# Three pieces of the key compression's weights split into places of their own

## Chip, core and metric

One core of a Trainium2 chip runs the whole kernel. The metric is device time in microseconds from launch to end, as a median of runs. Beside it there is one profiled execution, from which all rows below come.

## The reference

One decoder layer over 512 tokens of width 1024, in float32. A normalised input is projected once; the columns of that projection feed an HGRN2 group of heads (a gated linear recurrence) and a sparse-attention group with three branches: compressed, selected and window keys. Both results go through one output projection, then a gated convolutional FFN of width 2816 and a last norm. The part that matters here is the compression of keys and values and what runs next to it:

```python
def compress_blocks(kv, pe, w1, w2):
    ...
    blk = kv[:, tok] + pe[:, None, :].astype(kv.dtype)
    blk = blk.transpose(0, 3, 1, 2, 4).reshape(B, G, n_cmp, CMP_BLOCK * D)
    return jax.nn.silu(blk @ w1) @ w2
...
    kc = compress_blocks(kc_raw, pe_k, ck_w1, ck_w2)
    vc = compress_blocks(kv_heads(v_cmp), pe_v, cv_w1, cv_w2)
```

`w1` is 2048 x 256, so each of the two compressions multiplies a 2 MB weight.

## The kernel before

**Products in two halves.** Every float32 weight is split into a high part in the fp32r type and a low part, the remainder. ScalarE makes the high part (line 129), VectorE the low part (line 130), and TensorE then runs three products (high-high, high-low, low-high) that it adds up in PSUM. In the compression the two parts of the activations lie side by side in one operand, so there are two products for each step (lines 445 and 446).

**Places.** A piece of a weight is 128 x 1024 floats (512 KB). `stage` loads it into one of four places `ws` through SP's DMA queue. `hilo` takes one of four places `wh` and one of four places `wl`. A place `ws` comes free when VectorE's `wl` is done; places `wh` and `wl` come free when TensorE's last product with them is done. So no load starts until an earlier piece is split, and no piece is split until an earlier one is multiplied.

**Names of the pieces**, in the order of the program: KC and VC (keys and values to be compressed, line 400), q0a and q0b (`proj_q(0)`, line 373), K0 (`proj_k(0)`, line 386), then ck0 to ck3 (`compress(0)`, line 441), hi0 and hi1 (`hgrn_nat`, line 621), cv0 to cv3 (`compress(1)`), and then the pieces of the work that fills gaps in the attention. KC to K0 take 24 products of 512 columns each; ck and cv take 8 products of 256 columns for a piece; hi0 and hi1 together 96 products of 256 columns.

**Other tiles.** `xx` is a shifted copy of the roped keys or the values, made by eight DMAs on SP's queue (lines 409 and 410); `xa` and `xs` (lines 418 and 421) are made from it by VectorE and ScalarE and are the left operand of the compression. `khl` (line 384) holds the keys of one group of heads and is filled by four DMAs on SP's queue (line 394). Tag `k` has two places of 128 x 2048 floats: they hold in turn `wvh` (twice, the weights of the values), the `khl` of group 0 and of group 1, and later `kg` of the recurrence. `sg0` and `sg1` are the gates of the HGRN2 group, `mixn0` to `mixn3` the results of the attention.

**Order.** The program's text gives each instruction a priority, and a scheduler that runs while the kernel is built lays down one fixed order for each engine and queue: the first in the text among those that it finds ready. The places of a tag are handed out while it does so. The order around the change is written by hand:

```python
ck, cv, hi = compress(0), compress(1), hgrn_nat(OFF_HI, 0)
for st in (ck, ck, hi, ck, hi, cv, ck, cv, hi, cv, hi, cv):
    next(st, None)
```

Of the kernel before, what the change touches and what calls it, by code (L numbers as in the profile page):

```python
# [8 lines left out]
F32 = mybir.dt.float32  # L9
F32R = mybir.dt.float32r  # L10
# [7 lines left out]
P = 128  # L18
# [3 lines left out]
NT = SEQ // P  # L22
# [7 lines left out]
WSLOT = 1024  # L30
# [25 lines left out]
def kernel(ctx: ExitStack, tc: tile.TileContext, ins, consts: bass.AP, out: bass.AP):  # L56
# [66 lines left out]
    def hilo(n):  # L123
        hi = wp.tile([P, WSLOT], F32R, name="wh", tag="wh")[:, :n]
        lo = wp.tile([P, WSLOT], F32R, name="wl", tag="wl")[:, :n]
        return hi, lo
# [2 lines left out]
        nc.scalar.activation(dst_hi, src, AF.Copy)  # L129
        nc.vector.tensor_tensor(dst_lo, src, dst_hi.bitcast(F32), ALU.subtract)  # L130

    def chunk(src, shape):
        n = shape[0] * shape[1]
        st = stage(src, shape)
        hi, lo = hilo(n)
        split(hi, lo, st)
        v = lambda a: a.rearrange("p (a b) -> p a b", a=shape[0])
        return v(hi), v(lo)
# [69 lines left out]
    with ExitStack() as fc:  # L208
        fp = fc.enter_context(tc.tile_pool(name="fp", bufs=1))
# [159 lines left out]
        def proj_q(g):  # L369
            qt2 = [qp.tile([P, 2, SEQ], F32R, name=f"qs{g}{b}", tag="q") for b in range(2)]  # L370
            qs[g] = [qt2[b // 2][:, b % 2, :] for b in range(NB)]
            for pair in range(2):
                wh, wl = chunk(w_in[:, :, OFF_NQ + 256 * g + P * pair:OFF_NQ + 256 * g + P * (pair + 1)], (KT, P))
                y = rope(proj_T(wh, wl))
                qq = fp.tile([P, 2, SEQ], F32R, name="qq", tag="junk", bufs=3)
                nc.scalar.activation(qq[:, 0, :], y, AF.Copy, scale=0.125)
                nc.vector.scalar_tensor_tensor(qq[:, 1, :], y, 0.125, qq[:, 0, :].bitcast(F32), ALU.mult, ALU.subtract)
                for e in range(2):
                    for r in range(2):
                        nc.sync.dma_start(qt2[pair][r * HD:(r + 1) * HD, e, :].bitcast(F32), qq[e * HD:(e + 1) * HD, r, :].bitcast(F32))  # L380
                yield

        def proj_k(g):
            khl = fp.tile([P, 2, 2, SEQ], F32R, name=f"khl{g}", tag="k", bufs=2)
            kh[g], kl[g] = khl[:, 0], khl[:, 1]
            st = stage([w_in[:, :, off + g * HD:off + (g + 1) * HD] for off in (OFF_KS, OFF_KW)], (KT, P))
            hi, lo = hilo(DM)
            split(hi, lo, st)
            y = rope(proj_T(*(a.rearrange("p (a b) -> p a b", a=KT) for a in (hi, lo))))
            th = fp.tile([P, 2, SEQ], F32R, name="th", tag="junk", bufs=3)  # L390
            split(th[:, 0, :], th[:, 1, :], y)
            for br in range(2):
                for r in (0, HD):
                    nc.sync.dma_start(khl[r:r + HD, :, br, :].bitcast(F32), th[br * HD:(br + 1) * HD].bitcast(F32))
            yield
# [3 lines left out]
        for which, off in enumerate((OFF_KC, OFF_VC)):  # L399
            wh, wl = chunk(w_in[:, :, off:off + P], (KT, P))  # L400
# [29 lines left out]
        own = sm.tile([P, NB], F32, name="own", bufs=1)  # L430
        nc.vector.tensor_reduce(own, ident.rearrange("p (b n) -> p b n", b=NB)[:, :, 0:NCMP], AX.X, ALU.add)

        def compress(which):
            w1n, w2n = (("cmp_k_w1", "cmp_k_w2"), ("cmp_v_w1", "cmp_v_w2"))[which]
            w2 = fp.tile([P, 2, 2, HD], F32, name="w2", tag="w2", bufs=2)
            for r in range(2):
                nc.sync.dma_start(w2[:, :, r, :], ins[w2n][0].rearrange("(k p) d -> p k d", p=P))
            w1 = ins[w1n][0].rearrange("(j p) h -> p j h", p=P)
            hid = bank("pt")[:, :256]
            for c in range(4):  # L440
                wh, wl = chunk(w1[:, 4 * c:4 * c + 4, :], (4, 256))
                for j in range(4):
                    jj = 4 * c + j
                    lhs = kvx[which][jj // 8][:, jj % 8, :]
                    mm(hid, lhs, wh[:, j, :], jj == 0, False)
                    mm(hid, lhs, wl[:, j, :], False, jj == 15)
                if c == 1:
                    yield
            hs = fp.tile([P, 256], F32, name="hs", tag="asq")[:2 * NC2, :]
            nc.scalar.activation(hs, hid[:2 * NC2, :], AF.Copy)  # L450
            yield
            hp = bank("pt")[:, :2 * NC2]
            for m in range(2):
                mm(hp[:, m * NC2:(m + 1) * NC2], hs[:, m * P:(m + 1) * P], cst[:2 * NC2, C_CMB:C_CMB + NC2], True, True)
            th = sm.tile([P, 2 * NC2], F32, name="cth", tag="cth", bufs=2)
            nc.scalar.activation(th, hp, AF.Tanh, scale=0.5)
            nc.vector.scalar_tensor_tensor(th, th, 1.0, hp, ALU.add, ALU.mult)
            if which:
                thr = hw("thr").rearrange("p (a b n) -> p a b n", a=4, b=NB)
                nc.gpsimd.memset(thr, 0.0)  # L460
                nc.scalar.activation(thr[:, :, :, 0:NCMP], th.rearrange("p (a n) -> p a n", a=4).unsqueeze(2).broadcast_to([P, 4, NB, NCMP]), AF.Copy)
            yield
            act = [th[:, m * NC2:(m + 1) * NC2] for m in range(2)]
            if which == 0:
                o = bank("pt")[:, :2 * NCMP]
                for m in range(2):
                    mm(o, w2[:, m].rearrange("p a d -> p (a d)"), act[m], m == 0, m == 1)
                o3 = o.rearrange("p (g n) -> p g n", g=2)
                nc.scalar.activation(kc[:, :, 0, 0:NCMP], o3, AF.Copy, scale=0.5)
                nc.vector.scalar_tensor_tensor(kc[:, :, 1, 0:NCMP], o3, 0.5, kc[:, :, 0, 0:NCMP].bitcast(F32), ALU.mult, ALU.subtract)  # L470
            else:
                for g in range(2):
                    o = bank("pt")[:, :HD]
                    for m in range(2):
                        mm(o, thr[:, 2 * m + g].rearrange("p b n -> p (b n)"), w2[:, m, 0, :], m == 0, m == 1)
                    vf = fp.tile([P, NB, HD], F32, name="vf", tag="asq")
                    nc.vector.scalar_tensor_tensor(vf, o.unsqueeze(1).broadcast_to([P, NB, HD]), 0.5, own.unsqueeze(2).broadcast_to([P, NB, HD]), ALU.mult, ALU.mult)
                    split(vc[:, g, :, 1, :], vc[:, g, :, 0, :], vf)


        mixn = [fp.tile([P, 512], F32, name=f"mixn{t}") for t in range(NT)]


        scaled = {}
# [131 lines left out]
        vh, sg = {}, {}  # L616
# [3 lines left out]
        def hgrn_nat(off, c0):  # L620
            ws = [chunk(w_in[:, 4 * a:4 * a + 4, off + c0:off + c0 + 256], (4, 256)) for a in range(2)]
            pair = c0 // 256
            if off == OFF_HI:
                vh[pair] = fp.tile([P, NT, 256], F32, name=f"vh{pair}", tag="junk", bufs=3)
            else:
                sg[pair] = fp.tile([P, NT, 256], F32, name=f"sg{pair}")
            for t in range(NT):
                o = bank("mm")[:, :256]
                tk = slice(t * P, (t + 1) * P)
                for k in range(KT):  # L630
                    wh, wl = ws[k // 4]
                    mm3(o, hh[:, k, tk], hl[:, k, tk], wh[:, k % 4, :], wl[:, k % 4, :], k == 0, k == KT - 1)
                if off == OFF_HI:
                    nc.scalar.activation(vh[pair][:, t, :], o, AF.Copy)
                else:
                    th = unit("gth")[:, :256]
                    nc.scalar.activation(th, o, AF.Tanh, scale=0.5)
                    nc.vector.scalar_tensor_tensor(sg[pair][:, t, :], th, 1.0, o, ALU.add, ALU.mult)
                yield
# [117 lines left out]
        def attention(g):  # L757
            units = [(g, i, r) for i in TILES[g] for r in ((3, 0) if i < 2 else (1, 2, 0))]
            for u, n in zip(units, FILL[g]):
                pr = softmax_parts(*u)  # L760
                if todo:
                    weighted(*todo.pop())
                todo.append((*u, pr))
                every(itertools.islice(filler, n))
            weighted(*todo.pop())
# [8 lines left out]
# [3 lines that stand above are left out]
        for st in (ck, cv, hi):  # L777
            every(st)
        filler = itertools.chain(proj_q(1), proj_k(1), hgrn_nat(OFF_HG, 0), hgrn_nat(OFF_HG, 256), hgrn_fq(0), hgrn_nat(OFF_HI, 256), hgrn_fq(1))
        attention(0)  # L780
        attention(1)
        every(filler)
# [331 lines left out]
```

## Time and profile before

| | |
|---|---|
| median of 3 runs | 692.2 us (690.06 to 693.33) |
| profiled execution, its own time | 691.09 us |
| its span, first to last instruction | 689.3 us |
| TensorE busy | 672.1 us, 98% of the span |
| mean granted TensorE clock | 0.994 |

The profiled execution lies 1.1 us under the median, within the spread of the runs. 1.8 us of its time lie outside the span. Matmuls are pipelined, so a matmul's duration overlaps the next one's; what a product costs in a dense stream is the distance from one start to the next.

### The profile page before, as it was taken

How to read it: one execution, taken by the hardware profiler on the slowest of the kernel's cores; microseconds unless marked ns; L12 is line 12 of the kernel's file. 1: busy time of each engine (PE TensorE's matmuls, PEld its weight loads, DVE VectorE, ACT ScalarE, POOL GpSimd, SP SyncE). 2: the span in 40 equal slices, each digit the busy share in tenths (PEclk: the TensorE clock that was granted, in tenths of full speed). 3: DMA queues.
4: the chain of work that ended last, by engine and by line, in shares of the span. 5: the costliest groups of instructions: out<-in, count | busy, mean ns of one | idle time of the engine just before them, and what ended most of it. 6: DMA issues, size and time to landing. Idle time of an engine off the chain costs nothing.

```text
span 689.3 us, 11311 instructions
## 1 busy us (share of the span) xinstructions
PE 672.1 (98%) x4357; PEld 589.8 (86%) x4357; DVE 530.1 (77%) x930; ACT 392.4 (57%) x730; POOL 31.1 (5%) x82
## 2 busy tenths in 40 slices
PE   7999999999999999999999999999999999999995
PEld 4988878888888887887999898989989898989884
DVE  6878489887787678856886879788786878778665
ACT  6834587688878556335275464545445453645425
POOL 2000000000020121000000000000000000000001
PEclk9999999999999999999999999999999999999998
DMA  7947942320324312222231334334342333324303
GB/s 245 248 134 194 260 127 63 92 56 8 91 63 129 116 62 62 61 63 61 62 93 47 97 103 121 104 89 117 92 123 83 101 94 100 120 87 123 122 3 122
DMA packets 91142, 71.26 MB, mean 103 GB/s; under 512 B 8007, under 2 KB 78415, under 8 KB 91088
## 3 DMA queue, kind: packets, MB, share of 16 engines
q1 hardware_dynamic: 90800, 70.01, 35.3%
q8 instruction: 34, 0.56, 0.3%
q10 hardware_dynamic: 288, 0.52, 0.2%
q14 instruction: 20, 0.16, 0.1%
HBM read 63.18 MB, written 2.10 MB: 95 GB/s over the span
## 4 chain that ended last, share of the span: by engine, by line
PE 73%; DVE 12%; DMA 4%; ACT 4%; issue 3%; POOL 1%; SPq 1%; POOLq 0%; DVEq 0%; ACTq 0%
PE bmm L81 31%; PE bs L81 15%; PE bpt L81 15%; PE bo L81 8%; DVE wl L130 3%; PE bpt L565 2%; DMA ws<-in_ffn_w_up_dram 2%; POOL rs L110 1%; ACT wh L129 1%; DMA ws<-in_cmp_v_w_dram 1%; DVE x L993 1%; ACT y L1060 1%; DMA qs<-qq 1%; DMA xx<-y 1%; PE bpt L185 1%
## 5 line engine op out<-in xcount | busy, mean ns | idle before, releaser
L130 DVE TENSOR_TENSOR wl<-ws,wh 128x1024 fp32r<-128x1024 f32 x108 | 118.7, 1107 | 42.2 <-ACT wh L129 41.3
L129 ACT ACTIVATE wh<-ws 128x1024 fp32r<-128x1024 f32 x108 | 103.9, 964 | 60.1 <-PE bmm L81 21.4
L81 PE MATMUL bmm<-hTh,wh 128*128 128x256 f32 (+1 forms) x416 | 134.7, 324 | 0.0
L81 PE MATMUL bmm<-hTh,wl 128*128 128x256 f32 (+1 forms) x416 | 134.7, 324 | 0.0
L81 PE MATMUL bmm<-hTl,wh 128*128 128x256 f32 (+1 forms) x416 | 133.8, 322 | 0.6 <-DVE hTl L130 0.6
L81 PE MATMUL bs<-tt,wh 128*128 128x256 f32 x456 | 84.6, 284 | 0.2 <-ACT bs L961 0.2
L81 PEld LDWEIGHTS bmm<-hTl,wh 128*128 128x128 f32 x416 | 78.4, 189 | 6.6 <-DVE hTl L130 0.8
L81 PEld LDWEIGHTS bmm<-hTh,wl 128*128 128x128 f32 x416 | 78.4, 188 | 6.1 <-DVE wl L130 0.4
L81 PEld LDWEIGHTS bmm<-hTh,wh 128*128 128x128 f32 x416 | 78.4, 188 | 5.8
L129 ACT ACTIVATE wh<-s 128x1024 fp32r<-128x1024 f32 x38 | 40.4, 1064 | 58.8 <-PE bpt L81 24.8
L81 PEld LDWEIGHTS bs<-tt,wh 128*128 128x128 f32 x456 | 70.4, 188 | 2.3 <-ACT bs L961 0.4
L81 PE MATMUL bpt<-wh,ah 128*128 128x512 f32 (+1 forms) x179 | 70.4, 393 | 0.5 <-DVE x L993 0.5
L81 PE MATMUL bpt<-wl,ah 128*128 128x512 f32 (+1 forms) x179 | 70.0, 391 | 0.0
L81 PE MATMUL bpt<-wh,al 128*128 128x512 f32 (+1 forms) x179 | 70.0, 391 | 0.0
L81 PE MATMUL bs<-tt,wl 128*128 128x256 f32 x228 | 63.8, 280 | 0.0
L81 PE MATMUL bmm<-wh,hTh 128*128 128x256 f32 (+1 forms) x192 | 63.1, 330 | 0.2 <-DVE y L361 0.2
L81 PE MATMUL bmm<-wl,hTh 128*128 128x256 f32 (+1 forms) x192 | 62.7, 327 | 0.0
L81 PE MATMUL bmm<-wh,hTl 128*128 128x256 f32 (+1 forms) x192 | 61.9, 323 | 0.0
L130 DVE TENSOR_TENSOR wl<-s,wh 128x1024 fp32r<-128x1024 f32 x38 | 46.5, 1224 | 18.2 <-ACT wh L129 17.9
L110 POOL TENSOR_TENSOR rs<-ms,mhalf 128x4 f32<-128x4 f32 (+1 forms) x23 | 19.0, 828 | 587.9 <-DVE ms L108 587.9
L81 PEld LDWEIGHTS bs<-tt,wl 128*128 128x128 f32 x228 | 43.0, 189 | 0.0
L81 PEld LDWEIGHTS bpt<-wh,ah 128*128 128x128 f32 x179 | 33.6, 188 | 8.3 <-DVE x L993 1.3
(262 smaller groups left out, 1373.7 us busy)
## 6 DMA issues: line engine op xcount, KB each, us to landing
ws<-in_w_in_dram SPq DMA_DIRECT2D x22, 512.0 KB, 4.2
ws<-in_ffn_w_gate_dram SPq DMA_DIRECT2D x22, 512.0 KB, 4.0
ws<-in_ffn_w_up_dram SPq DMA_DIRECT2D x22, 512.0 KB, 4.3
ws<-in_ffn_w_down_dram SPq DMA_DIRECT2D x20, 512.0 KB, 3.7
ws<-in_w_o_dram SPq DMA_DIRECT2D x8, 512.0 KB, 3.4
ws<-in_cmp_k_w_dram SPq DMA_DIRECT2D x4, 512.0 KB, 4.6
qs<-qq SPq DMA_DIRECT2D x16, 128.0 KB, 3.4
ws<-in_cmp_v_w_dram SPq DMA_DIRECT2D x4, 512.0 KB, 6.1
```

What stands on the lines that cost most here:

```text
L81: return nc.tensor.matmul(o, lhsT, rhs, start=start, stop=stop, skip_group_check=True)
L110: nc.gpsimd.tensor_tensor(rs[:, :width], ms[:, :width], mhalf[:, :width], ALU.pow)
L129: nc.scalar.activation(dst_hi, src, AF.Copy)
L130: nc.vector.tensor_tensor(dst_lo, src, dst_hi.bitcast(F32), ALU.subtract)
L185: nc.tensor.transpose(pt[:, j * P:(j + 1) * P], self.y[:, c:c + P], ident)
L565: t = nc.tensor.transpose(pt[:, b * P:(b + 1) * P], srcs[b], ident)
L993: nc.vector.tensor_tensor(x_sb[t][:, hs], o, x_sb[t][:, hs], ALU.add)
L1060: nc.scalar.activation(y[:, HV[h]], y[:, HV[h]], AF.Copy, scale=rs)
```

## The change

The high and low parts of ck0, ck1 and ck2 no longer take places `wh` and `wl`. ck0 takes one place of a tag `sg` and one of a tag `mixn`; so does ck1; ck2 takes the two halves of a place of tag `k`. ck3 and all pieces of the value compression stay as they were. `sg0` and `sg1` get a common tag with two places, and the four `mixn` tiles become two tiles of double width in two places, made just before the attention. The bytes set aside are the same as before.

```diff
-    def chunk(src, shape):
+    def chunk(src, shape, room=None):
         n = shape[0] * shape[1]
         st = stage(src, shape)
-        hi, lo = hilo(n)
+        hi, lo = room or hilo(n)
         split(hi, lo, st)
...
+        def room(which, c):
+
+            if which or c == 3:
+                return None
+            if c == 2:
+                both = fp.tile([P, 2, WSLOT], F32R, name="wk", tag="k", bufs=2)
+                return both[:, 0], both[:, 1]
+            return [fp.tile([P, WSLOT], F32R, name="wk", tag=t, bufs=2) for t in ("sg", "mixn")]
+
         def compress(which):
...
-                wh, wl = chunk(w1[:, 4 * c:4 * c + 4, :], (4, 256))
+                wh, wl = chunk(w1[:, 4 * c:4 * c + 4, :], (4, 256), room(which, c))
...
-        mixn = [fp.tile([P, 512], F32, name=f"mixn{t}") for t in range(NT)]
+        mixn = []
...
-                sg[pair] = fp.tile([P, NT, 256], F32, name=f"sg{pair}")
+                sg[pair] = fp.tile([P, NT, 256], F32, name=f"sg{pair}", tag="sg", bufs=2)
...
+        for _ in range(2):
+            m2 = fp.tile([P, 2, 512], F32, name="mixn", tag="mixn", bufs=2)
+            mixn += [m2[:, 0], m2[:, 1]]
         attention(0)
```

## Rows read from the trace of the kernel before

**Rows 1.** Busy time by stretch of the compression and its neighbours: stretch in us from the span's start, its length, then busy us and instructions of each engine, granted clock, DMA share, GB/s.

```profile
30.00:45.00 15.00, 15.00 (x66) 12.09 (x65) 9.04 (x22) 4.81 (x8) 0.00 (x0) 1.00 0.71 195
45.00:60.00 15.00, 14.76 (x82) 12.51 (x80) 14.97 (x26) 8.28 (x12) 0.53 (x1) 1.00 0.49 137
60.00:65.00 5.00, 4.11 (x24) 3.81 (x24) 3.49 (x5) 1.82 (x3) 0.00 (x0) 0.78 0.85 241
65.00:70.00 5.00, 5.00 (x40) 5.00 (x39) 3.16 (x4) 1.95 (x5) 0.00 (x0) 0.88 0.69 154
```

**Rows 2.** TensorE's matmuls in order of time: start, us, line, output and inputs, moving operand, count; in brackets the idle time before and what ended it. `bpt<-wh,xs` is a product of a compression, `bmm<-wh,hTh` one of hi0 or hi1. From 55.42 to 59.05 there are 32 starts, from 62.74 to 66.28 there are 18.

```profile
55.42 0.28 PE L81 MATMUL bpt<-wh,xs 128*128 128x256 f32 x1
...
59.05 0.28 PE L81 MATMUL bpt<-wl,xs 128*128 128x256 f32 x1
59.16 0.40 PE L81 MATMUL bmm<-wh,hTh 128*128 128x256 f32 x2
59.80 0.66 PE L81 MATMUL bpt<-cst,hs 124*128 124x62 f32 x4 [0.24 <-ACT hs L450]
60.68 0.38 PE L81 MATMUL bmm<-wh,hTh 128*128 128x256 f32 x1 [0.22 <-DVE y L361]
61.73 0.35 PE L81 MATMUL bpt<-wh,xs 128*128 128x256 f32 x1 [0.67 <-issue]
61.92 0.28 PE L81 MATMUL bmm<-wl,hTh 128*128 128x256 f32 x1
...
62.74 0.36 PE L81 MATMUL bmm<-wh,hTl 128*128 128x256 f32 x1
...
66.28 0.28 PE L81 MATMUL bmm<-wl,hTh 128*128 128x256 f32 x1
...
76.93 0.28 PE L81 MATMUL bmm<-wl,hTh 128*128 128x256 f32 x1
77.69 0.39 PE L81 MATMUL bpt<-wh,xs 128*128 128x256 f32 x1 [0.48 <-ACT wh L129]
```

**Rows 3.** VectorE in order of time, same columns: the six low parts `wl` are those of ck0, ck1, ck2, ck3, hi0 and hi1, in this order; between them stand the last step of a rope (line 363; the one at 36.47 is that of KC) and the last splits of `xs`.

```profile
36.47 0.70 DVE L363 TENSOR_TENSOR y<-y,sh 128x512 f32<-128x512 f32 x1
39.68 1.23 DVE L130 TENSOR_TENSOR wl<-ws,wh 128x1024 fp32r<-128x1024 f32 x1 [2.52 <-ACT wh L129]
...
49.16 1.25 DVE L130 TENSOR_TENSOR xs<-xa,xs 128x496 fp32r<-128x496 f32 x2
...
50.93 1.22 DVE L130 TENSOR_TENSOR wl<-ws,wh 128x1024 fp32r<-128x1024 f32 x1
52.07 0.69 DVE L363 TENSOR_TENSOR y<-y,sh 128x512 f32<-128x512 f32 x1
52.67 1.22 DVE L130 TENSOR_TENSOR wl<-ws,wh 128x1024 fp32r<-128x1024 f32 x1
...
56.97 1.22 DVE L130 TENSOR_TENSOR wl<-ws,wh 128x1024 fp32r<-128x1024 f32 x1
...
60.54 1.21 DVE L130 TENSOR_TENSOR wl<-ws,wh 128x1024 fp32r<-128x1024 f32 x1
...
62.27 1.22 DVE L130 TENSOR_TENSOR wl<-ws,wh 128x1024 fp32r<-128x1024 f32 x1
```

**Rows 4.** ScalarE in order of time, same columns: high parts (line 129, `wh`): at 38.59 that of ck0, at 55.44 those of ck3 and hi0, at 64.40 that of cv1, at 69.79 that of cv2; and two that stand behind one (line 406 takes the values out of PSUM, `th` are the keys of group 0).

```profile
38.59 1.06 ACT L129 ACTIVATE wh<-ws 128x1024 fp32r<-128x1024 f32 x1 [4.54 <-PE bmm L81]
39.55 0.58 ACT L406 ACTIVATE y<-bmm 128x512 f32<-128x512 f32 x1
...
55.44 2.12 ACT L129 ACTIVATE wh<-ws 128x1024 fp32r<-128x1024 f32 x2 [2.01 <-PE bmm L81]
...
64.40 1.06 ACT L129 ACTIVATE wh<-ws 128x1024 fp32r<-128x1024 f32 x1 [2.61 <-DMA ws<-in_cmp_v_w_dram]
65.36 0.61 ACT L129 ACTIVATE th<-y 128x512 fp32r<-128x512 f32 x1
...
69.79 1.06 ACT L129 ACTIVATE wh<-ws 128x1024 fp32r<-128x1024 f32 x1 [0.36 <-PE bpt L81]
```

**Rows 5.** SP's queue in order of time: start, us from the first issue to the last of the row, line, what is loaded, count.

```profile
27.36 9.53 SPq L120 DMA_DIRECT2D ws<-in_cmp_k_w_dram  x4
37.23 0.54 SPq L409 DMA_DIRECT2D xx<-y  x1
...
43.21 9.38 SPq L120 DMA_DIRECT2D ws<-in_w_in_dram  x2
...
66.77 3.52 SPq L394 DMA_DIRECT2D khl<-th  x4
70.33 1.17 SPq L120 DMA_DIRECT2D ws<-in_cmp_v_w_dram  x1
```

**Rows 6.** DMA issues of the page: what is loaded, queue, count, KB each, median us from issue to landing.

```profile
ws<-in_cmp_k_w_dram SPq DMA_DIRECT2D x4, 512.0 KB, 4.6
```

**Rows 7.** The second filling of `khl`, for group 1, on SP's queue (columns as in rows 5), and the last products with the first filling on TensorE (columns as in rows 2).

```profile
122.53 3.73 SPq L394 DMA_DIRECT2D khl<-th  x4
...
126.11 0.63 PE L81 MATMUL bs<-khl,qs 128*128 128x256 f32 x4
```

**Rows 8.** First writes of the later owners of the other places: from the views of the tiles `sg` and `mixn` (engine, operation, count: duration ns min/median/max, first and last start us).

```profile
L638 DVE SCALAR_TENSOR_TENSOR sg<-gth,bmm x8: 410/417/422, 132.1 to 180.3; 128x256 f32<-128x256 f32 x8
L607 DVE TENSOR_TENSOR mixn<-on,rs x8: 424/425/427, 111.5 to 230.5; 128x256 f32<-128x256 f32 x8
```

## The prediction, made before the changed kernel was run

> **What bounds the kernel now.** I read the busy times by stretch first. TensorE is full from 30 to 59 us and again after 80; what it loses near the change lies between 59 and 78. The reader should see three things in the stretches [rows 1]: from 30 to 45 VectorE has 6.0 of 15 us free and ScalarE 10.2; from 45 to 60 VectorE has nothing free (14.97 of 15); from 60 to 65 TensorE is idle for 0.9 us and its mean granted clock is 0.78, then 0.88. So a jam on VectorE ends just ahead of TensorE's loss.
>
> TensorE's own rows tell what the loss is [rows 2]. The 32 products of ck0 to ck3 run without a gap, 31 distances in 3.63 us, 0.117 us each. Two products of hi0 follow, and then the stream breaks. The first product with a low part of hi0 starts at 61.92, because that low part is made only from 60.54 on [rows 3].
>
> Why is it so late? ScalarE's rows show ck0's high part waiting 4.54 us for a product, and those of ck3 and hi0 for another [rows 4]: a piece is not split until an earlier one has been multiplied. With four places, ck0 waits for VC's products, ck1 for q0a's, ck2 for q0b's, ck3 for K0's, and hi0 for ck0's at 56.5. The low parts of ck1, ck2 and ck3 thus fall at 50.93, 52.67 and 56.97, into the full stretch, and that of hi0 queues behind them and behind the ropes [rows 3]. SP's queue shows the next link: each low part frees a place `ws`, so the load of hi0 is issued at 43.21 and that of hi1 near the end of that row, 52.6, though four ck loads were issued by 36.9 [rows 5]. The later waits are echoes: cv3 is loaded at 70.33, behind the copies of `khl`, and TensorE waits for its split until 77.69 [rows 5, 2].
>
> **The change, part by part.**
>
> *Removed: the wait of three pieces for products.* ck0 to ck2 can be split when they have landed. Issues from 27.36 on and 4.6 us to landing [rows 5, 6] put the first landing at 32.0; the other two leave before the fourth (36.9) and so land before 41.5. Each low part takes VectorE 1.14 us (50.93 to the next start at 52.07) [rows 3]. No instruction is added; those of ck1 and ck2 (2.3 us) go from the full stretch into the 6.0 us that VectorE has free before 45, and so does that of ck3, because it can now take VC's place, free when ck0's high part starts before (38.59), instead of K0's at 55.44 [rows 1, 4]. Cost on the path: nothing, covered by this free time. If that were gone, they would stay where they are, and the gain with them.
>
> *What moves up.* Three low parts fewer ahead of hi0's and hi1's: 60.54 and 62.27 become at the latest 57.1 and 58.8, done by 60.0. hi0's is needed at 59.28 + 0.12 = 59.4, hi1's 12 products after the start at 59.16, at 60.6. It suffices, by 0.6 us for hi1 if VectorE's order stays. The loads come forward too: hi0 and hi1 need places `ws` that are free at about 35 to 38; the four cv loads then follow each low part in turn.
>
> *The gain, step by step* [rows 2].
> - The break: from 59.40, when the third product of hi0 was due, to 61.92 it is 2.52 us. In them TensorE does four small products (0.66) and two of 0.117: 2.52 - 0.66 - 0.23 = 1.6 us.
> - The slow stretch: from 62.74 to 66.28 the clock is at its lower level, 1.2 of 2.4 GHz, after the broken stretch before it. 17 distances take 3.54 us; at 0.117 they would take 1.99. That is 1.55 us. I take it that without the break the clock does not fall; the bound on the other side is that it falls anyway, a gain of 0 here.
> - The wait for cv3: due at 76.93 + 0.12 = 77.05, started at 77.69: 0.65 us. It goes if the load leaves before the copies of `khl`; else 0.
>
> Sum 3.8 us. By listed idle time alone it would be 1.1 + 0.5 us and by the clock column (0.22 + 0.12) x 5 = 1.7 us, together 3.3; by the gap's full length with none of its products subtracted, 4.7. I take 3.8, since distances hold what idle time leaves out.
>
> *Added: other owners of the new places.* `mixn` is first written at 111.5 and `sg` at 132.1 [rows 8]; ck0 and ck1 are multiplied by about 57.3. Cost 0, with 54 us of cover. The merged `mixn` tiles are written by VectorE alone, in its order: 0.
>
> *Added: a third claim on the two places `k`.* ck2's place must be back before the keys of group 1 are copied in at 122.53, 65 us later [rows 7]. If places were handed out strictly in turn, those keys would have to wait for group 0's, last read from 126.11 to about 126.7 [rows 7]: 4.2 us for the copies and for what then waits for them. One row speaks against that: cv2's high part starts at 69.79, released by a product of a compression [rows 4]. In turn its place would have been hi0's, which takes part in the last 24 products of hi, and these still run at 76.93 [rows 2]. So places go to whoever finds one free, and I take 0, bound 4.2.
>
> *The rest.* After 80 TensorE stays full in the attention, and the FFN is a fixed sequence. I carry the gain to the end. The scheduler lays down the order anew from these earlier times, though; the waits of the later stages are a few tenths each, so I allow 2 us either way.
>
> The Trainium skill bears on one point. The row is cv1's high part: ScalarE waits 2.61 us for its load, and the keys' `th`, which do not need it, start only behind it [rows 4]. "TensorE: Matmul & The Clock Gate" (Part 1, on engine queue depths) says that ScalarE and VectorE are strict FIFOs. The trace agrees (2.61 us), and by that rule an early split that is laid ahead of the values' copy (line 406) while its piece is still under way would hold that copy; by it the sum would lose up to 2.61 us wherever no slack is left.
>
> **The rivals.**
>
> *A, the sum above:* 692.2 - 3.8 = 688.4. In the profile's own time 691.1 - 3.8 = 687.3.
>
> *B, half of it:* the break shrinks, but a shorter one is left, and the clock falls after it, or the attention's new order gives back about 2 us. For it: hi1's margin of only 0.6 us, and one split waiting behind another's load as at 64.40. 3.8 - 1.8 = 2.0: 690.2.
>
> *C, nothing:* the places are not what hi0 waits for. VectorE puts the same work (hi0's and hi1's ropes and splits) into the time won, or the third claim on `k` gives back 4.2. Against it: the 4.54 us ahead of ck0's split are put down to a product, and cv2 was served out of turn. 692.2, to 692.6.
>
> *D, slower:* SP's queue. The loads of hi0 and hi1 can now be ready before the eight copies of `xx`, which were issued from 37.23 on, before them [rows 5]. If they are laid ahead of the copies, `xx` is held while each waits for its place and moves. Two loads at 4.6 us [rows 6] hold `xx` for up to 9.2 us. `xs` is done at 50.4 [rows 3] and needed at 55.42 [rows 2], so the first 5.0 us cost nothing; from there on every microsecond delays the compression. 9.2 - 5.0 = 4.2 us, with the old break still there: 696.4. Against it: transfers overlap (four loads were issued in 9.5 us, and at most 0.71 of the DMA engines were busy from 30 to 45 [rows 1]), so 2 to 4 us is likelier than 9.2.
>
> **How the numbers follow.** A 0.58, B 0.18, C 0.14, D 0.10. The predicted time is A's, 688.4. A's own range is 685.5 to 690, from the 2 us of the later order and the terms at 3.3 to 4.7. The range with 8 in 10 reaches from 685 to 692.3: all of A but its lowest part, B, and the better half of C. 0.5% of 692.2 is 3.5 us, about what a measurement of this kernel can tell from no change, so 688.7 is the line. A is just below it, and its own range lies 3.2 us below that line and 1.3 above: I put 0.43 of its 0.58 below: faster 0.43. Slower (over 695.7) is nearly all of D: 0.09. No change is the rest of A and D with B and C: 0.48.
>
> **What would show it.** Right: ck0's to ck2's high parts start before 40; VectorE has less than 6 us free from 30 to 45; hi0's low part is done before 59; no idle time on TensorE between 59 and 62, clock 1.00 from 60 to 70; cv3's load is issued before the copies of `khl`; `khl` for group 1 is not later than before. Wrong: the same gap at another place, a load ahead of `xx` on SP's queue with `xs` done after 55, or ScalarE waiting for a load with line 406 or a split of `xs` behind it.

## The result, and the profile after

The changed kernel takes 687.8 us (median of 6 runs, 687.35 to 689.06), the kernel before, beside it, 691.8 us (690.06 to 693.33): ratio 0.9947 with the interval [0.9931, 0.9964], 4.0 us by the medians. The profiled execution of after took 687.35 us with a span of 685.6, against 691.09 and 689.3: 3.7 us.

Busy time by stretch of after, columns as in [rows 1]:

```profile
30.00:45.00 15.00, 15.00 (x66) 12.09 (x65) 10.55 (x25) 6.63 (x9) 0.00 (x0) 1.00 0.74 201
45.00:60.00 15.00, 15.00 (x84) 12.86 (x83) 14.96 (x27) 6.48 (x9) 0.53 (x1) 1.00 0.63 189
60.00:65.00 5.00, 4.74 (x41) 4.57 (x40) 3.74 (x6) 2.12 (x4) 0.00 (x0) 1.00 0.81 242
65.00:70.00 5.00, 4.98 (x42) 4.78 (x42) 1.83 (x3) 1.94 (x4) 0.00 (x0) 1.00 0.95 234
```

VectorE has 4.45 us free from 30 to 45 (before 6.0), TensorE has lost 0.26 us from 60 to 65 (before 0.89), and the granted clock is 1.00 throughout (before 0.78 and 0.88).

TensorE in order of time, columns as in [rows 2]; `wk` are the new places:

```profile
55.83 2.06 PE L81 MATMUL bpt<-wk,xs 128*128 128x256 f32 x16
57.72 0.28 PE L81 MATMUL bmm<-wh,hTh 128*128 128x256 f32 x1
57.84 0.28 PE L81 MATMUL bmm<-wl,hTh 128*128 128x256 f32 x1
...
63.84 0.28 PE L81 MATMUL bmm<-wl,hTh 128*128 128x256 f32 x1
64.38 0.36 PE L81 MATMUL bpt<-wk,xs 128*128 128x256 f32 x1 [0.26 <-ACT wk L129]
...
74.97 0.28 PE L81 MATMUL bpt<-wl,xs 128*128 128x256 f32 x1
...
76.37 0.34 PE L81 MATMUL bs<-khl,qs 128*128 128x384 f32 x1
```

After ck0 and ck1 comes hi0, its low part included, without a gap. The one wait is that of 64.38, for ck2. The last product of the values' compression starts at 74.97, and only then the keys' `khl` products begin; before, seven products of cv3 lay behind the first of those.

The splits tell where this comes from. ScalarE's high parts, columns as in [rows 4]:

```profile
32.33 1.04 ACT L129 ACTIVATE wk<-ws 128x1024 fp32r<-128x1024 f32 x1
33.39 1.06 ACT L129 ACTIVATE wh<-ws 128x1024 fp32r<-128x1024 f32 x1
34.35 1.05 ACT L129 ACTIVATE wk<-ws 128x1024 fp32r<-128x1024 f32 x1
39.22 0.60 ACT L406 ACTIVATE y<-bmm 128x512 f32<-128x512 f32 x1 [3.82 <-PE bmm L81]
41.56 1.06 ACT L129 ACTIVATE wh<-ws 128x1024 fp32r<-128x1024 f32 x1 [1.74 <-DMA ws<-in_cmp_k_w_dram]
45.39 1.13 ACT L129 ACTIVATE xs<-xa 128x496 fp32r<-128x496 f32 x2 [2.77 <-DVE xa L418]
...
50.22 1.99 ACT L129 ACTIVATE wh<-ws 128x1024 fp32r<-128x1024 f32 x2
...
63.19 1.05 ACT L129 ACTIVATE wk<-ws 128x1024 fp32r<-128x1024 f32 x1
```

ck0 and ck1 are split at 32.33 and 34.35, with K0 between them, and ck3 at 41.56. The pair at 50.22 is hi0 and hi1. The last row is ck2, at 63.19, behind both.

VectorE's low parts, columns as in [rows 3] (ck0 and ck1, ck3, hi0, hi1, ck2):

```profile
37.47 2.37 DVE L130 TENSOR_TENSOR wk<-ws,wk 128x1024 fp32r<-128x1024 f32 x2
42.66 1.22 DVE L130 TENSOR_TENSOR wl<-ws,wh 128x1024 fp32r<-128x1024 f32 x1 [2.82 <-ACT wh L129]
...
51.92 1.24 DVE L130 TENSOR_TENSOR wl<-ws,wh 128x1024 fp32r<-128x1024 f32 x1
53.66 1.24 DVE L130 TENSOR_TENSOR wl<-ws,wh 128x1024 fp32r<-128x1024 f32 x1
...
64.27 1.22 DVE L130 TENSOR_TENSOR wk<-ws,wk 128x1024 fp32r<-128x1024 f32 x1 [0.53 <-ACT wk L129]
```

hi0's low part stands at 51.92 instead of 60.54, hi1's at 53.66 instead of 62.27.

SP's queue, columns as in [rows 5] and [rows 7]:

```profile
27.61 9.67 SPq L120 DMA_DIRECT2D ws<-in_cmp_k_w_dram  x4
37.63 0.54 SPq L409 DMA_DIRECT2D xx<-y  x1
...
43.54 1.10 SPq L120 DMA_DIRECT2D ws<-in_w_in_dram  x2
44.73 8.82 SPq L120 DMA_DIRECT2D ws<-in_cmp_v_w_dram  x2
...
61.88 0.58 SPq L120 DMA_DIRECT2D ws<-in_cmp_v_w_dram  x1
63.81 3.79 SPq L394 DMA_DIRECT2D khl<-th  x4
...
119.60 3.45 SPq L394 DMA_DIRECT2D khl<-th  x4
```

The copies `xx` keep their place ahead of the loads of hi0 and hi1. These two leave within 1.10 us instead of 9.38; hi0's own load leaves no earlier (43.54, before 43.21), so what hi0 gained is the place for its split, not its load. And cv3's load leaves at 61.88, ahead of the `khl` copies, instead of at 70.33, behind them. Group 1's `khl` comes at 119.60 (before 122.53).

### The profile page after: what moved, and what is told of

It is laid out like the page before. It is cut to its first block, busy times and chain, and to the rows that moved or that the text cites. A ratio compares the mean times of both kernels' runs of the same rounds, so it can differ in the third digit from the quotient of the medians.

```text
span 685.6 us, 11311 instructions
## 1 busy us (share of the span) xinstructions
PE 669.9 (98%) x4357; PEld 588.1 (86%) x4357; DVE 530.1 (77%) x930; ACT 391.6 (57%) x730; POOL 31.2 (5%) x82
## 4 chain that ended last, share of the span: by engine, by line
PE 76%; DVE 11%; ACT 4%; DMA 3%; issue 2%; POOL 1%; POOLq 0%; ACTq 0%; DVEq 0%; SPq 0%
PE bmm L81 32%; PE bpt L81 16%; PE bs L81 16%; PE bo L81 8%; DVE wl L130 2%; PE bpt L574 2%; DMA ws<-in_ffn_w_up_dram 1%; POOL rs L110 1%; ACT wh L129 1%; DMA ws<-in_w_in_dram 1%; DVE x L1005 1%; ACT y L1072 1%; DMA ws<-in_cmp_k_w_dram 1%; PE bpt L185 1%; ACT pn L528 1%
## 5 line engine op out<-in xcount | busy, mean ns | idle before, releaser
L130 DVE TENSOR_TENSOR wl<-ws,wh 128x1024 fp32r<-128x1024 f32 (+1 forms) x105 | 115.0, 1102 | 39.9 <-ACT wh L129 39.8
L129 ACT ACTIVATE wh<-ws 128x1024 fp32r<-128x1024 f32 (+1 forms) x105 | 100.4, 961 | 56.1 <-PE bs L81 16.3
```

## Experiments

Starts before the compression vary with the execution: the first compression product lies between 55.12 and 57.55 in the traces below, while the 120 products ahead of it, from the first of the projection KC on, take 28.07 to 28.09 us in every trace. So the traces are compared from that first compression product on. "Stage" is the time from it to the first `khl` product. "Rest" is the time from the same first compression product to the last product with `ah`, near the kernel's end, so it holds the stage (us, worked out from the starts in TensorE's rows).

| trace | first product | stage | rest |
|---|---|---|---|
| before | 55.42 | 22.97 | 626.41 |
| before_again | 55.12 | 22.04 | 624.91 |
| e0_names | 56.16 | 22.60 | 626.44 |
| after | 55.83 | 20.54 | 622.26 |
| after_again | 55.93 | 20.47 | 622.08 |
| e1_ck0_ck1 | 56.69 | 20.97 | 621.23 |
| e2_ck2_alone | 56.26 | 20.18 | 622.38 |
| e3_ck0_alone | 56.52 | 21.59 | 622.24 |
| e4_k_in_use_early | 57.26 | 20.15 | 622.63 |
| e5_break_filled | 56.61 | 26.42 | 627.86 |
| e6_filled_and_cv3_first | 57.55 | 24.42 | 624.51 |
| e7_cv3_first | 56.74 | 24.26 | 624.66 |
| e7_again | 56.04 | 24.52 | 624.52 |
| e8_values_too | 55.82 | 20.93 | 621.90 |

The stage alone can mislead where other work changes sides of its end (the seven products above; in e6 and e7 `khl` is moved back), so verdicts go by the rest and by the medians.

**The names alone, and the change once more.** e0 is after with tags and merged tiles, but with no piece moved:

```diff
-            if which or c == 3:
+            if True:
                 return None
```

> The new tags alone: sg in one tag with two places, mixn as two double tiles, but all four key pieces still take places wh and wl. T and S: no piece is split earlier, so the time is that of the kernel before, ratio 0.999 to 1.001, with the slow stretch from 62.7 to 66.3. A rival by which the merged tiles or their addresses matter: a difference of 0.5% or more.

Measured: 691.32 us, ratio 0.9998 [0.9988, 1.0008]; rest 626.44, as before. The break and the lower clock are there (0.85 and 0.81 in 60 to 65 and 65 to 70). So the merged tiles by themselves change nothing that the interval can tell (0.8 us at most), and the effect comes from moving pieces.

> The changed kernel itself, beside the others on one chip. Theory T (the gain is that hi0 and hi1 are split before TensorE needs them; the stretch of 2.5 us without their products, the slow clock behind it and the late cv3 go together): 3.8 us under the kernel before, ratio 0.9945. Rival S (each piece that no longer waits brings its share, a third each): the same here.

Measured: 687.31 us, 0.9947 [0.9928, 0.9965]; the same gain, and the same rest as after to 0.2 us.

**Which piece pays?** Three versions of after that move fewer pieces; the lines that replace `if which or c == 3` are

```diff
+            if which or c >= 2:
...
+            if which or c != 2:
...
+            if which or c != 0:
```

for e1 (ck0 and ck1), e2 (ck2 alone) and e3 (ck0 alone).

> Only ck0 and ck1 get places of their own (sg and mixn); ck2 takes a place wh and wl as before. T: ck2 takes VC's place (free at 38.6), ck3 q0a's (44.2), hi0 q0b's (49.8), hi1 K0's (55.4), all in time but for hi1, whose low part is due at 60.6 and can be made by about 58 to 60: the whole gain, 3.5 to 3.8 us, ratio 0.9945 to 0.995; ck2's split before 45 instead of at 63 as in the changed kernel. S: two thirds, 2.5 us, ratio 0.9964.

> Only ck2 gets a place of its own (tag k); ck0 and ck1 as before. T: one claim fewer on wh and wl, so ck3 takes q0b's place (49.8), hi0 K0's (55.4) and hi1 ck0's (56.4): hi0's low part by about 58, just in time, and ck2's products come late behind those of hi; the clock stays at its upper level from 60 to 70 and 2.5 to 3.8 us are gained, ratio 0.9945 to 0.9964. S: a third, 1.3 us, ratio 0.998, with the slow stretch still there.

> Only ck0 gets a place of its own. T: ck1, ck2, ck3 take VC's, q0a's and q0b's places, hi0 K0's (55.4), hi1 that of ck1 (57.3): hi0's low part at about 57 to 59, just in time, hi1's at about 60: 2.5 to 3.8 us gained, ratio 0.9945 to 0.9964, if no new break comes at hi1. S: a third, 1.3 us, ratio 0.998.

Measured: e1 687.00 us, 0.9934 [0.9917, 0.9951]; e2 687.18 us, 0.994 [0.9924, 0.9957]; e3 688.04 us, 0.9947 [0.9933, 0.996]. Each gives what all three give; a share for each piece does not hold. e2 is the instructive one. ScalarE's row of the moved piece, the low part of hi0 on VectorE, TensorE's one wait from 55 to 80, and SP's later queue, in e2:

```profile
65.90 1.05 ACT L129 ACTIVATE wk<-ws 128x1024 fp32r<-128x1024 f32 x1
```

```profile
57.86 1.22 DVE L130 TENSOR_TENSOR wl<-ws,wh 128x1024 fp32r<-128x1024 f32 x1
```

```profile
59.13 0.39 PE L81 MATMUL bmm<-wl,hTh 128*128 128x256 f32 x1 [0.60 <-DVE wl L130]
```

```profile
65.05 3.63 SPq L394 DMA_DIRECT2D khl<-th  x4
68.72 1.14 SPq L120 DMA_DIRECT2D ws<-in_cmp_v_w_dram  x1
```

The moved piece is split at 65.90, later than before the change, and ck0 still waits for a product as before. What pays is that the piece no longer takes a turn at the four places `wh` and `wl`, so that those behind it come one turn earlier: hi0's low part at 57.86 instead of 60.54, with a wait of 0.60 us left. And cv3's load stands behind `khl`, as before, but earlier (68.72 against 70.33, which is 2.45 us when both are counted from the first compression product), and TensorE has no wait for it: its time counts, not its rank.

**ck2 early.** e4 is after, with ck2's place made and touched (one column set to zero by GpSimd) ahead of the keys' projection, so that it is used before `khl`:

```diff
+        early_k = fp.tile([P, 2, WSLOT], F32R, name="wk", tag="k", bufs=2)
+        nc.gpsimd.memset(early_k[:, 0, 0:1].bitcast(F32), 0.0)
```

> The changed kernel, with one addition: a column of ck2's place is cleared by GpSimd ahead of the code that fills khl of group 0, so that the place is used first by ck2. T, with the reading that a tag's places are handed out in the order of first use in the text: ck2's high part moves from 63.2 to before 40, TensorE's wait for it at 64.4 (0.4 us in starts) goes, 0.2 to 0.5 us under the changed kernel. Rival (ck2 is late for another reason, its load or ScalarE's order): ck2's high part stays at about 63 and the time is that of the changed kernel.

Measured: 688.81 us, 0.9965 [0.995, 0.998]. ck2 is now split at 37.48. So neither its load nor ScalarE made ck2 late in after: its place was claimed behind `khl` in the program's text, and with the two turned round ck2 comes early. e4 moves the making of the tile and its first use together, so which of the two sets the order is not shown. That gains nothing: the rest is 622.63 (after 622.26), with a new wait of 0.77 us at 78.51 for the values' compression. Of the 1.5 us by which e4's median lies above after's this explains 0.4; its trace starts the compression 1.43 us later than after's, and whether that is the rule for e4 one trace doesn't tell.

**Are the three terms of the sum independent?** e5 is the kernel before with twelve products of zeros into an unused bank, put behind ck3's last product, which fill the break and compute nothing:

```diff
-                    mm(hid, lhs, wl[:, j, :], False, jj == 15)
+                    end = mm(hid, lhs, wl[:, j, :], False, jj == 15)
+                    if which == 0 and jj == 15:
+                        for _ in range(12):
+                            behind(mm(warm, zero[:, :P], zero, True, True).ins, end.ins)
```

> The kernel before, with 12 products of zeros (bf16, 512 columns, into an unused bank) laid behind the last product of ck3; nothing else is changed, and their results are not used. They take about 2.6 us of TensorE and stand where it waited for hi0's low part. T: the break is filled, so the clock does not fall: 1.00 from 60 to 70, 1.0 to 1.6 us under the kernel before, ratio 0.9977 to 0.9986. Rival (the clock falls in this stretch anyway, or from what ran long before): granted clock about 0.8 from 60 to 70 and no gain, or a loss of up to 1 us.

Measured: 691.91 us, 1.0003 [0.9991, 1.0014]; the gain that was expected of the clock did not come. The trace is of an execution of 693.75 us, the longest of the twelve. Busy time by stretch of e5, then its zero products and its wait on TensorE:

```profile
60.00:65.00 5.00, 4.97 (x32) 3.39 (x31) 4.62 (x6) 1.66 (x3) 0.00 (x0) 1.00 0.87 246
65.00:70.00 5.00, 5.00 (x45) 5.00 (x44) 2.87 (x3) 2.40 (x5) 0.00 (x0) 1.00 0.73 177
...
75.00:80.00 5.00, 2.99 (x22) 2.79 (x21) 1.23 (x1) 1.89 (x3) 0.00 (x0) 0.90 1.09 306
80.00:85.00 5.00, 5.00 (x32) 4.87 (x32) 2.83 (x4) 2.60 (x5) 0.00 (x0) 0.76 1.04 255
```

```profile
60.35 2.76 PE L81 MATMUL bo<-zero 128*128 128x512 bf16 x12
...
78.56 0.39 PE L81 MATMUL bpt<-wh,xs 128*128 128x256 f32 x1 [2.01 <-ACT wh L129]
```

The zero products take 2.42 us of TensorE's stream (60.35 to the next start, 62.77) and give the break's time to nobody: hi0's first low-part product comes 6.46 us after the first compression product, before 6.50. So e5 tests the clock's term alone. The clock stays up behind the filled break, and TensorE arrives earlier at cv3, which is not there: 2.01 us of waiting (0.48 before), and the clock falls there instead. cv3's first product starts 21.95 us after the first compression product, before 22.27. What the clock gave was taken back by the load.

e6 is e5 with the first `khl` copies moved behind cv3's load on SP; e7 has that move alone, without the zeros. Besides the lines below, `proj_k` pauses ahead of its copies, and they are tied behind the last load issued (left out here):

```diff
-        every(proj_k(0))
+        k0 = proj_k(0)
+        next(k0)
...
+            if j == 7:
+                every(k0)
```

> The kernel before, with the twelve zero products of e5_break_filled in the break after the products of ck3, and also with khl's two loads of the first group moved behind the load of cv3 on SP's queue. If the terms of the sum stand in series (the break, the slow stretch behind it and cv3's late load being the same microseconds, of which the last one open decides): with both closed TensorE is busy without a break from 55 to 80, the granted clock is 1.00 there, and the kernel is 2 to 3.5 us faster than before, ratio 0.995 to 0.997 (the twelve products cost about 2.6 us that the missing wait and clock have to pay first, so the low end is 0.9985). If cv3's load was not what held e5, or the twelve products eat the whole gain: ratio 0.999 to 1.001, and another wait stands at 75 to 85.

> The kernel before with khl's two loads of the first group behind cv3's load on SP's queue and nothing else. By the sum of the prediction (its third term by itself): the wait of 0.65 us at 77.69 goes, the break at 59 to 62 and the lower clock from 62 to 66 stay: 0.3 to 0.7 us faster, ratio 0.999 to 0.9995. If the load chain alone was the cause: the whole gain, ratio 0.9945. If khl's later load holds the attention behind it: 0.5 to 1 us slower, ratio 1.001.

Measured: e6 690.98 us, 0.9987 [0.9974, 1.0]; e7 690.4 us, 0.9986 [0.9972, 1.0]. e6 by stretch:

```profile
60.00:65.00 5.00, 5.00 (x33) 3.48 (x32) 5.00 (x9) 2.60 (x4) 0.00 (x0) 1.00 0.77 213
65.00:70.00 5.00, 4.94 (x42) 4.73 (x42) 2.37 (x3) 2.02 (x4) 0.00 (x0) 1.00 1.06 299
70.00:75.00 5.00, 5.00 (x45) 5.00 (x44) 3.63 (x6) 2.61 (x4) 0.00 (x0) 1.00 0.94 209
75.00:80.00 5.00, 4.91 (x42) 4.71 (x41) 0.82 (x2) 1.94 (x4) 0.00 (x0) 1.00 1.04 263
```

With break and load both dealt with, TensorE is full at full clock from 60 to 80, as the reading in series says. By time e6 is inconclusive: its ratio lies just outside the 0.9985 that this reading allowed at worst, with an interval that holds both readings. Its rest is 1.90 us shorter than that of before with twelve zero products in it, which take 2.4 us of the stream: together 4.3 us, about what after gains against the same trace (4.15). By the medians it is 0.3 + 2.4 = 2.7 us of after's 4, so that both together give the whole gain is not shown. e7, with the break left, is 1.75 us shorter by its rest and 0.9 by the medians, with 0 to 1.9 for the interval; the 0.65 us of the one wait lie inside it.

**Does the clock fall each time?** In e7's trace the break was there, and the clock did not fall. So before and e7 were each traced a second time.

> The kernel before, unchanged, for a second trace. If the break at 59 to 62 brings TensorE's clock down each time: 62 to 66 at a granted clock of 0.5 again, as in the first trace and in e0_names. If it falls in some executions only: the same break of about 1.6 us with the clock at 1.00 behind it, as in e7_cv3_first, and the stage about 1.5 us shorter.

> e7_cv3_first once more, for a second trace. If the full clock behind its break (65 to 70 at 1.00) was a matter of that execution: 63 to 67 at 0.5 this time. If the order of the loads has to do with it: 1.00 again, while before_again shows 0.5.

Measured: 689.29 us for before_again, 689.83 us for e7_again, one run each. Stretches 60 to 65 and 65 to 70 of before_again, e7 and e7_again, in this order:

```profile
60.00:65.00 5.00, 4.33 (x35) 4.01 (x35) 3.06 (x4) 2.48 (x4) 0.00 (x0) 1.00 0.98 250
65.00:70.00 5.00, 4.59 (x38) 4.25 (x37) 3.57 (x5) 2.04 (x4) 0.00 (x0) 1.00 0.74 159
```

```profile
60.00:65.00 5.00, 4.02 (x30) 3.49 (x29) 4.76 (x7) 1.95 (x4) 0.00 (x0) 1.00 0.85 254
65.00:70.00 5.00, 4.67 (x40) 4.47 (x39) 3.04 (x4) 2.23 (x4) 0.00 (x0) 1.00 1.04 282
```

```profile
60.00:65.00 5.00, 3.95 (x24) 3.44 (x23) 4.32 (x6) 1.60 (x3) 0.00 (x0) 0.84 0.89 243
65.00:70.00 5.00, 5.00 (x37) 5.00 (x37) 3.15 (x4) 2.10 (x4) 0.00 (x0) 0.82 1.03 273
```

The same kernel does the one and the other: the order of the loads does not decide it. Nor does the chip alone: before_again and e7_again ran on the same one. Of five traces with the unfilled break (before, e0, e7_again; before_again, e7) the first three have the fall. Their breaks are not quite equal: from the first compression product to hi0's first low-part product it is 6.50, 6.61 and 6.65 us in these three, 6.29 and 6.34 in the two without the fall. Whether this difference decides it, five traces don't tell. And where the clock stays up, waits come in: TensorE's row in before_again that has no counterpart in before,

```profile
67.43 0.38 PE L81 MATMUL bpt<-wl,xs 128*128 128x256 f32 x1 [0.41 <-DVE wl L130]
```

and in e7 two waits for low parts, 0.9 us, which e7_again has not. e7 and e7_again end within 0.14 us of each other, counted from the first product, one with the full clock and one with the fall. before and before_again differ by 0.93 us in the stage, where 1.55 were put down to the fall, and by 1.50 by the end of the rest. Like with like, moving cv3's load gives 1.89 us between the two traces with the fall (before, e7_again) and 0.25 us between the two without (before_again, e7).

**More of the same.** e8 moves ck0 and ck1, and of the values' pieces cv0 and cv1 too:

```diff
-            if which or c == 3:
+            if c >= 2:
```

> ck0 and ck1 in the places of sg and mixn as in e1_ck0_ck1, ck2 by wh and wl, and the first two pieces of the values' compression in the places of sg and mixn as well. If the stage of the two compressions is bound by TensorE from 45 to 80 once one piece is out of the way: nothing more to gain, ratio 0.993 to 0.995, like e1. If places still hold the values' pieces: the values end about 1 us earlier, ratio 0.991 to 0.9925. If the earlier splits push ck3 or hi0 back on VectorE: a break opens at 55 to 62 again, ratio 0.995 to 0.998.

Measured: 688.58 us, 0.9954 [0.9938, 0.9971]. Nothing more is gained: from 60 to 75 TensorE was full in e1 already. No version here is shown to beat after; e1's interval overlaps with after's.

## Why the prediction was right

688.4 us was forecast, 687.8 measured, with "faster" the right side, if by little. Step by step:

- *The mechanism held, with hi0 at the centre.* The places were what held it: one piece less in the queue for them suffices (ck2 in e2, ck0 in e3), and names alone do nothing (e0). hi0's and hi1's low parts came earlier than the bounds of 57.1 and 58.8, at 51.92 and 53.66.
- *"ck0 to ck2 can be split when they have landed" failed for ck2.* It went from 49.79 to 63.19 on ScalarE. Behind it lies the step on the third claim: "places go to whoever finds one free" was drawn from cv2's split out of turn [rows 4] and does not hold for a tag whose other user stands earlier in the program. e4 shows that this order decides. The step's price of 0 stood all the same, since TensorE took up hi0 and hi1 first; ck2's lateness cost the wait of 0.26 us at 64.38.
- *The sum was right in size, in part by luck, and wrong in its working.* 3.8 us was forecast for the stage. Counted from the first compression product, the stage is shorter by 22.97 - 20.54 = 2.43 us, and the seven products of cv3 no longer behind it are 7 x 0.117 = 0.82: 3.25. What comes behind the stage adds 626.41 - 622.26 - 3.25 = 0.90, inside the 2 us allowed for the later order, and the start took back 0.41. 3.25 + 0.90 - 0.41 = 3.74, the 3.7 of the spans. That this comes so near to 3.8 is luck: the stage gave less than forecast, 0.90 that no term of the sum named made up for it, and the trace compared with happened to have the fall of the clock (the spans of before_again and after differ by 687.5 - 685.6 = 1.9).
- *The three terms are not independent.* They were added as if each could be had by itself. They stand in series in front of one late chain of loads: keep the clock up by filling the break, and the wait for cv3 grows from 0.48 to 2.01 us (e5); where the clock stays up by itself, waits for low parts come in (before_again, e7). By itself the clock's 1.55 came to nothing in e5. The change moves the chain itself, its splits and its loads; that this is why the terms could be had together is argued from e5 and from e6's trace, not shown by e6's time.
- *The clock term* took a fall that happens in some executions for a fixed one. Against before_again, whose clock stayed up, after's rest is 2.65 us shorter instead of 4.15, as far as one trace of each tells. The ratio of the medians mixes both kinds in a proportion that was not measured.
- *The rivals.* D: `xx` was not held [SP's queue above]; the last splits of `xs` start at 50.15 and the products need them at 55.83. C's third claim: group 1's `khl` is 2.9 us earlier, no later. B: neither a shorter break nor a new order gave back anything that the trace shows.
- *ScalarE's order.* Of the splits of ck and hi only ck3's waits for its load, 1.74 us at 41.56, and it stands behind line 406, not ahead of it. It cost nothing: TensorE has no wait from 14 us to 64.38. "TensorE: Matmul & The Clock Gate" of the Trainium skill says that ScalarE is a strict FIFO (Part 1, on engine queue depths). This wait does not test it: the next entry, a split of `xs`, was released by VectorE's `xa` only at 45.39.

## What to carry to other kernels

Where several pieces take turns at a few places, find the piece that TensorE waits for and count the turns ahead of it: here taking one piece out of the queue ahead of it (ck0 or ck2) moved it up enough, and the piece taken out could itself come late. Before adding up stalls that follow one another on one engine, ask whether one late chain feeds them all; if so, removing one may only uncover the next, as in e5, and what has to move is the chain. A place shared with another user was handed out here in the order of the program's text, so look where that other user stands.

## What was not expected of the hardware

The fall of TensorE's clock behind the break of 1.6 us differs from execution to execution: the same instructions, a break that differs by 0.2 to 0.4 us, and a granted clock of 0.78 and 0.88 in one trace of before, 1.00 in the other; 1.00 in e7 and 0.84 and 0.82 in e7_again. "TensorE: Matmul & The Clock Gate" of the Trainium skill (Part 1, the note on the warm-up) says of the start of a kernel that the number of slow products varies from run to run; the traces here show such a variation in mid-kernel, 0 or about 17 products. The fall itself went with a broken stretch in which no single listed idle time was above 0.67 us, and in e5 with one wait of 2.01 us.
